# Gate and up products of a transformer block: weight blocks in the array and all 256 tokens moving, with norm pieces issued one tile ahead

## The chip, the core and the metric

The kernel runs on one core of one Trainium2 chip. A core has a matrix engine (PE in the profile; its loads of the stationary operand are listed apart as PEld), a vector engine (DVE), a scalar engine (ACT), a general engine (POOL) and a sync engine (SP), which here issues the transfers from memory. The metric is the device time of one execution in microseconds (us); lower is better. A matrix product holds one operand of 128x128 in the array (the stationary one, loaded by a LDWEIGHTS) and streams the other through it (the moving one, up to 512 columns); its result goes to an accumulator in PSUM.

## The reference

It is one block of a conformer-like transformer on 256 tokens of width 2048, all in float32:

```python
h = modulate(rms_norm(x, ffn1_norm), sh1, sc1)
x = x + 0.5 * g1[:, None, :] * swiglu(h, ffn1_w_gu, ffn1_w_down)
h = modulate(rms_norm(x, mix_norm), shm, scm)
y = hybrid_mixer(h, cos, sin, w_in, ...)        # differential attention and a causal convolution
x = x + gm[:, None, :] * y
h = modulate(rms_norm(x, ffn2_norm), sh2, sc2)
x = x + 0.5 * g2[:, None, :] * swiglu(h, ffn2_w_gu, ffn2_w_down)

def swiglu(h, w_gu, w_down):
    gu = jnp.einsum('bsd,df->bsf', h, w_gu)
    g, u = jnp.split(gu, 2, axis=-1)
    return jnp.einsum('bsf,fd->bsd', jax.nn.silu(g) * u, w_down)
```

The nine vectors of shifts, scales and gates come from one more product, of silu(c) with a matrix of 2048 x 18432 (`w_ada`). The inner width of swiglu is 5632.

## The kernel before

**Precision.** Every large product is made of three products of 32-bit operands: each operand is split into a high part that the array takes exactly and the rest (hi and lo), and hi x hi, hi x lo and lo x hi are added up in one accumulator (`mm3`, L311 to L316). Weights come from memory in tiles of 512 rows by 512 columns (1 MB, in `raw`); `w_tile` (L276) lets ACT make the high half (L293, `whi`) and DVE the rest (L295, `wlo`).

**A product tile.** `mm_tile` (L318) takes one weight tile. The activations are stationary: for each of the tile's 4 blocks of 128 rows and each of the 2 blocks of 128 tokens, `mm3` loads a 128x128 block of activations and moves 512 weight columns past it, three times: 24 instructions of 512 columns for one tile. There are 176 tiles of gate and up weights (22 chunks of 256 gate and 256 up columns, 4 tiles each, two FFNs), 88 of the down projections, 40 of `w_in` and 16 of `w_out`: 320 in all, 7680 instructions.

**Gate and up, then down.** `ffn` (L434) first takes the tiles of the first 512 rows for all chunks (`stage_a`, copied out by ACT at L461), since the norm of those rows is ready first; then some chunks further (`again`, `early`), and last the rest of each chunk. `finish` (L568) adds the parts of a chunk on DVE, applies SiLU on ACT, multiplies gate by up on DVE, and then has PE transpose the result, 4 blocks of 128x128 per chunk (L576), since the down product needs the inner columns on the partitions; ACT and DVE split the transposed result (L326, L327). `finish` of a chunk is issued after the first tile of the next chunk. The down products (L619 to L650) make 4 column groups of 11 tiles; the last `HOLD_DN` = 2 tiles of the last group are held so that the first 128 tokens come to an end before the others, and `evac` (L609) of these runs beside the products of the rest.

**Norms.** The normalized activations come in 4 pieces of 512 columns for each 128 tokens. `piece` (L396) scales on ACT (L364), and one tile later, or when a product first asks for it (`act`), `complete` (L409) lets PE transpose (L370), DVE or ACT apply scale and shift (L418, L421), and ACT and DVE split (L422, L423). In the FFNs `pieces` issues a piece once the modulation columns for it are there; in the mixer a piece is issued just before the first tile that needs it (L986).

**Order.** Each engine runs its instructions in a fixed order, which the framework's scheduler draws from the order of the code. The columns of `w_ada` are a transfer of 1 MB each and a multiply-and-sum on DVE (L180); the table `DUE` (L47) and the shares in the calls of `ffn` say how many of them lie between the weight tiles. `after_tiles` puts a step off by a number of tiles. `ORDER` (L48) is the order of the tiles of `w_out`.

Of the kernel before, what the change touches and what calls it, by code (L numbers as in the profile page):

```python
# [24 lines left out]
P = 128  # L25
# [21 lines left out]
DUE = ((19, 8), (63, 16), (110, 24), (150, 32))  # L47
ORDER = [(0, 0), (1, 0), (0, 1), (1, 1), (2, 0), (2, 1)] + [(n, pc) for pc in (2, 3) for n in range(3)]  # L48
# [25 lines left out]
def block_kernel(ctx: ExitStack, tc: tile.TileContext, x_in, pos_in, w_ada, small, w_gu1, w_dn1,  # L74
# [250 lines left out]
    def split_from_psum(tp, hi, lo):  # L325
        nc.scalar.copy(out=hi, in_=tp)  # L326
        nc.vector.tensor_sub(out=lo, in0=tp, in1=hi.bitcast(F32))  # L327
# [101 lines left out]


    HOLD = 3
    HOLD_DN = 2

    def ffn(st, w_gu, w_dn, gate_base, ada_a, ada_b, nxt, again, early, early_3):  # L434
# [20 lines left out]

        def stage_a(c, w, accs, ts, n=4):
            mm_tile(accs, w, act, 0, True, True, ts, (0, n))
            if parts[c] is None:
                parts[c] = blk([P, NT, 512])
            for t in ts:  # L460
                last_part[0] = nc.scalar.copy(out=parts[c][:, t, :], in_=accs[t])  # L461
# [10 lines left out]
        if not st.done:  # L472

            raws, begun = st.begin_both(), [0]
            ws = {}

            def load(i):
                cs = LOADS[i]
                if ext[cs[0]] == 1:
                    ws.update(zip(cs, w_first(cs)))  # L480
                else:
                    ws[cs[0]] = w_tile(w_gu[cs[0], 0], False, (0, ext[cs[0]]), ext[cs[0]] < 4)

            for c in range(NCH):
                ext[c] = EXT[c] if c < len(EXT) else 4
            def begin_ready():
                while begun[0] < 4 and base + 2 * begun[0] + 2 <= ada_next[0]:
                    st.tile(raws[begun[0]], tmp([P, S]), (begun[0], slice(0, S)))
                    begun[0] += 1

            first_modulation(lambda n: load(0) if n == 3 else None)
            begin_ready()
            for i in range(len(LOADS) + AHEAD):
                if i < len(LOADS):
                    if i:
                        load(i)
                    with tc.issue_after(w_dma[0].ins):
                        if i < len(FIRST_ADA):
                            ada_until(ada_next[0] + FIRST_ADA[i])
                            rows[0] += ext[LOADS[i][0]] * len(LOADS[i])  # L500
                        else:
                            ada_a_share(ext[LOADS[i][0]])
                        begin_ready()
                if i >= AHEAD:
                    cs = LOADS[i - AHEAD]
                    assert begun[0] >= ext[cs[0]]
                    for c in cs:
                        stage_a(c, ws[c], [acc_tile() for _ in range(NT)], (0, 1), ext[c])
                    pieces()
        else:  # L510
            first = [(c, w_tile(w_gu[c, 0], c > 0), [acc_tile() for _ in range(NT)]) for c in range(3)]
            for t in range(NT):
                for c, w, accs in first:
                    stage_a(c, w, accs, (t,))
            with tc.issue_after(st.last.ins):
                ada_a_share(12)
            for c in range(3, NCH):
                w = w_tile(w_gu[c, 0])
                stage_a(c, w, [acc_tile() for _ in range(NT)], (0, 1))
                ada_a_share(4)  # L520
                pieces()
# [6 lines left out]
        def add_part(c, accs):  # L528
            for t in range(NT):
                nc.vector.tensor_add(out=parts[c][:, t, :], in0=accs[t], in1=parts[c][:, t, :])  # L530

        start_of = [0] * NCH
        for g in again:
            w = w_tile(w_gu[g, 0], False, (ext[g], 4))
            accs = [acc_tile() for _ in range(NT)]
            mm_tile(accs, w, act, 0, True, True, (0, 1), (ext[g], 4))
            ext[g] = 4
            add_part(g, accs)
            ada_a_share(3)
        for i_g, g in enumerate(early):  # L540
# [5 lines left out]
            for c in g:  # L546

                accs[c] = [acc_tile() for _ in range(NT)]
                begun_[c] = ext[c] < 4
                if ext[c] < 4:  # L550
                    w = w_tile(w_gu[c, 0], False, (ext[c], 4))
                    mm_tile(accs[c], w, act, 0, True, False, (0, 1), (ext[c], 4))
                    ada_a_share(4 - ext[c])
                    ext[c] = 4
            for c in g:
                upto = 3 if c in early_3 else 2
                for pc in range(1, upto):
# [3 lines left out]
                    mm_tile(accs[c], w, act, 4 * pc, pc == 1 and not begun_[c], pc == upto - 1)  # L561
# [6 lines left out]
        def finish(c, accs):  # L568
            p = parts[c]
# [8 lines left out]
            split_from_psum(tp, a[:, 0], a[:, 1])  # L578
# [4 lines left out]
        for g in groups:  # L583
            accs = {c: [acc_tile() for _ in range(NT)] for c in g}
            for i, (pc, ks) in enumerate(segments(g[0], start_of[g[0]], 4)):
                ada_until(base + 8 * pc + 8)
                pieces(last_part[0])
                for c in g:
                    w = w_tile(w_gu[c, pc], False, ks)
                    mm_tile(accs[c], w, act, 4 * pc, i == 0, pc == 3, (0, 1), ks)  # L590
# [17 lines left out]

        def evac(n, accs, ts=(0, 1)):  # L609
            for t in ts:  # L610
                m = tmp([P, 512])
# [8 lines left out]
        for n in range(4):  # L620
            accs = [acc_tile() for _ in range(NT)]
            held = []
            for pc in range(11):
                hold = n == 3 and pc >= 11 - HOLD_DN
                w = w_tile(w_dn[n, pc], hold and pc == 10)
# [94 lines left out]


    ffn(norm1, w_gu1, w_dn1, 32, (0.78, 32), (0.8, 104), norm_m, AGAIN, EARLY, EARLY_3)


# [139 lines left out]
    def attn_av(g, qb, hh_):  # L864
# [10 lines left out]
        if hh_ == 3:  # L875
# [22 lines left out]
            after_tiles(1, rest)  # L898
# [80 lines left out]
    for t in range(NT):  # L979
        for c, w, accs in first:  # L980
            mm_tile(accs, w, act, 0, True, False, (t,))
    for ci in range(10):
        p0 = 1 if ci < HOLD else 0
        accs = first[ci][2] if ci < HOLD else [acc_tile() for _ in range(NT)]
        for pc in range(p0, 4):
            for t in range(NT):  # L986
                st.piece(pc, t)
# [45 lines left out]
    for i, (n, pc) in enumerate(ORDER):  # L1033
# [105 lines left out]
```

## Time and profile before

| | |
|---|---|
| median of 3 runs | 1875.45 us (1874.09 to 1875.72) |
| the profiled execution | 1871.77 us |
| its span, first to last instruction | 1870.0 us |
| granted TensorE clock, mean | 0.996 |
| DVE busy | 1436.1 us (77%) |
| ACT busy | 917.8 us (49%) |
| memory traffic | 495.93 MB, mean 265 GB/s |

The profile is of one execution. An instruction's row has its line in the code, engine, operation, output and inputs by the program's names, partitions x elements, the count, and after the bar the busy time in us, the mean of one in ns and the idle time of its engine ahead of it with what ended it. The end of a product is modelled, and products overlap in the array, so their pace is read from the distances of their starts and not from their durations. A timeline row has the start and the duration in us, the engine, the line, and in brackets a wait and what ended it. "x4" merges four rows that follow each other.

### The profile page before, as it was taken

To read this page: it belongs to the slowest core of one execution; us is meant where nothing else is said; L and a number is where in the kernel's file an instruction comes from. 1 tells how busy PE (TensorE), PEld (TensorE's weight loads), DVE (VectorE), ACT (ScalarE), POOL (GpSimd) and SP (SyncE) were. 2 spreads that over 40 slices of the span, in tenths; PEclk is the share of its full clock that TensorE was granted. 3 is DMA by queue.
4 is the path that set the end of the run, shared out by engine and by line. 5 is a ranking of instruction groups with operands and counts; after the bars stand their busy time and mean duration, and the time that the engine had idled before them with its cause. 6 is when DMAs were issued, how large, how long until landed. Compare 5 with 4: busy or idle time off the path is not lost.

```text
span 1870.0 us, 21989 instructions
## 1 busy us (share of the span) xinstructions
PE 1836.9 (98%) x8303; PEld 1512.4 (81%) x8303; DVE 1436.1 (77%) x1902; ACT 917.8 (49%) x1390; POOL 31.3 (2%) x29
## 2 busy tenths in 40 slices
PE   7999999999999999999999999999999999999999
PEld 5778888888887888788888788887888888888887
DVE  7788969999888788769899688788877755544443
ACT  6654344444444434654787455664444444433332
POOL 0000000000000000000110000000000000000000
PEclk9999999999999999999999999999999999999999
DMA  9887978988889899635444476888777755555562
GB/s 383 320 323 275 361 261 310 339 315 333 328 332 352 326 376 355 256 133 189 174 152 142 151 280 271 332 318 336 259 286 276 285 197 180 192 213 206 199 213 79
DMA packets 72586, 495.93 MB, mean 265 GB/s; under 512 B 8176, under 2 KB 8352, under 8 KB 15008
## 3 DMA queue, kind: packets, MB, share of 16 engines
q1 hardware_dynamic: 72480, 494.53, 70.8%
q8 instruction: 65, 1.06, 0.2%
q14 instruction: 41, 0.34, 0.0%
HBM read 492.37 MB, written 2.12 MB: 264 GB/s over the span
## 4 chain that ended last, share of the span: by engine, by line
PE 91%; DVE 3%; DMA 3%; ACT 1%; issue 1%; POOL 0%; SPq 0%; POOLq 0%; ACTq 0%; DVEq 0%
PE acc L315 29%; PE acc L316 29%; PE acc L314 29%; DMA blk<-in_w_gu_dram 1%; PE tp L576 1%; DVE wlo L295 1%; DMA raw<-in_w_ada_dram 1%; PE acc L834 1%; DVE blk L742 1%; DMA raw<-in_w_dn_dram 1%; DVE raw L180 0%; PE tp L370 0%; ACT whi L293 0%; PE tp L909 0%; POOL rs L141 0%
## 5 line engine op out<-in xcount | busy, mean ns | idle before, releaser
L293 ACT CAST whi<-raw 128x1024 fp32r<-128x1024 f32 (+1 forms) x609 | 632.4, 1047 | 765.8 <-PE acc L316 607.2
L314 PE MATMUL acc<-whi,blk 128*128 128x512 f32 x2464 | 963.7, 394 | 6.5 <-ACT blk L379 2.7
L315 PE MATMUL acc<-wlo,blk 128*128 128x512 f32 x2464 | 964.6, 391 | 5.1 <-DVE wlo L295 5.1
L295 DVE TENSOR_TENSOR wlo<-raw,whi 128x1024 fp32r<-128x1024 f32 (+1 forms) x609 | 730.0, 1211 | 309.1 <-ACT whi L293 306.9
L316 PE MATMUL acc<-whi,blk 128*128 128x512 f32 x2464 | 962.2, 391 | 0.6 <-DVE blk L381 0.5
L315 PEld LDWEIGHTS acc<-wlo,blk 128*128 128x128 f32 x2464 | 464.5, 188 | 103.8 <-DVE wlo L295 9.8
L314 PEld LDWEIGHTS acc<-whi,blk 128*128 128x128 f32 x2464 | 464.1, 189 | 104.3 <-ACT whi L293 3.4
L316 PEld LDWEIGHTS acc<-whi,blk 128*128 128x128 f32 x2464 | 463.9, 188 | 99.1 <-DVE blk L381 2.0
L180 DVE CUSTOM_DVE_ANT_0 raw<-raw,c_bc 128x2048 f32<-128x2048 f32 x142 | 324.3, 2284 | 10.0 <-DMA raw<-in_w_ada_dram 9.5
L742 DVE SCALAR_TENSOR_TENSOR blk<-blk,cst,blk 128x255 f32<-128x255 f32 (+14 forms) x240 | 96.3, 458 | 0.0
L461 ACT COPY blk<-acc 128x512 f32<-128x512 f32 x88 | 49.9, 591 | 51.1 <-PE acc L316 49.0
L572 DVE TENSOR_TENSOR blk<-acc,blk 128x512 f32<-128x512 f32 x88 | 56.9, 682 | 1.7 <-PE acc L316 1.6
L314 PE MATMUL acc<-blk,blk 128*128 128x512 f32 x96 | 38.4, 403 | 2.1 <-ACT blk L422 2.1
L315 PE MATMUL acc<-blk,blk 128*128 128x512 f32 x96 | 38.0, 400 | 0.2 <-DVE blk L295 0.2
L316 PE MATMUL acc<-blk,blk 128*128 128x512 f32 x96 | 37.6, 396 | 0.0
L573 ACT ACTIVATE blk<-blk 128x256 f32<-128x256 f32 x88 | 32.8, 410 | 5.4 <-DVE blk L572 5.4
L574 DVE TENSOR_TENSOR blk<-blk 128x256 f32<-128x256 f32 x88 | 33.9, 417 | 1.4 <-ACT blk L573 1.4
L612 DVE TENSOR_TENSOR tmp<-acc,blk 128x512 f32<-128x512 f32 x16 | 10.7, 686 | 27.7 <-PE acc L316 27.7
L295 DVE TENSOR_TENSOR blk<-raw,blk 128x1024 fp32r<-128x1024 f32 x24 | 28.8, 1219 | 2.9 <-ACT blk L293 2.9
L327 DVE TENSOR_TENSOR blk<-tp,blk 128x512 fp32r<-128x512 f32 x44 | 29.9, 683 | 0.5 <-ACT blk L326 0.2
L421 ACT ACTIVATE tmp<-tp,ada,scales 128x128 f32<-128x128 f32 x48 | 18.9, 460 | 20.9 <-DVE scales L222 14.5
L530 DVE TENSOR_TENSOR blk<-acc,blk 128x512 f32<-128x512 f32 x36 | 23.8, 685 | 6.5 <-PE acc L316 6.4
(144 smaller groups left out, 682.3 us busy)
## 6 DMA issues: line engine op xcount, KB each, us to landing
raw<-in_w_gu_dram SPq DMA_DIRECT2D x161, 1024.0 KB, 5.4
raw<-in_w_ada_dram SPq DMA_DIRECT2D x142, 1024.0 KB, 6.3
raw<-in_w_dn_dram SPq DMA_DIRECT2D x88, 1024.0 KB, 5.0
raw<-in_w_in_dram SPq DMA_DIRECT2D x40, 1024.0 KB, 4.8
raw<-in_w_out_dram SPq DMA_DIRECT2D x16, 1024.0 KB, 4.7
raw<-in_w_gu_dram SPq DMA_DIRECT2D x8, 768.0 KB, 6.0
blk<-in_w_gu_dram SPq DMA_DIRECT2D x10, 512.0 KB, 13.9
blk<-gate_line SPq DMA_DIRECT2D x6, 512.0 KB, 6.6
```

Source lines behind the costliest of these rows:

```text
L180: nc.vector.tensor_tensor_reduce(out=raw, in0=raw, in1=c_bc, scale=1.0, scalar=0.0, op0=ALU.mult, op1=ALU.add, accum_out=ada_cols[g][:, j ...
L293: nc.scalar.copy(out=hi[:, :m, :], in_=rw)
L295: nc.vector.tensor_sub(out=lo[:, :m, :], in0=rw, in1=hi[:, :m, :].bitcast(F32))
L314: nc.tensor.matmul(acc, ah, wh, start=start, stop=False)
L315: nc.tensor.matmul(acc, ah, wl, start=False, stop=False)
L316: nc.tensor.matmul(acc, al, wh, start=False, stop=stop)
L327: nc.vector.tensor_sub(out=lo, in0=tp, in1=hi.bitcast(F32))
L461: last_part[0] = nc.scalar.copy(out=parts[c][:, t, :], in_=accs[t])
L572: nc.vector.tensor_add(out=p[:, t, :], in0=accs[t], in1=p[:, t, :])
L573: nc.scalar.activation(out=p[:, t, :256], in_=p[:, t, :256], func=AF.Silu)
L574: nc.vector.tensor_mul(out=p[:, t, 256:], in0=p[:, t, :256], in1=p[:, t, 256:])
L742: nc.vector.scalar_tensor_tensor(out=y[:, d:], in0=u, scalar=w, in1=y[:, d:], op0=ALU.mult, op1=ALU.add)
```

## The change

`mm_tile_wide` and `mm3_wide` are new: the weight tile is cut into 128x128 blocks, each of them is loaded into the array, and all 256 tokens move. A tile then takes 48 instructions of 256 columns instead of 24 of 512; an accumulator holds gate or up columns as [128 columns, 2 blocks, 256 tokens]. All of the first FFN and chunks 3 to 21 of the second go this way (164 of the 176 tiles); chunks 0 to 2 of the second FFN stay as before. `finish` then needs no transposes in 41 of the 44 chunks. Beside that:

- `act_wide` asks for a norm piece of both token blocks at once; `pieces` is called in two more places, and the mixer issues the next piece ahead of each of its first tiles.
- `HOLD_DN` is 3, `DUE` has the columns of `w_ada` a little earlier, the share behind it is 0.78 for 0.8.
- The order of the `w_out` tiles is plain (row group by row group), and the transposes of the second half of the heads are put off by two tiles.
- `evac_last`: the last 128x512 block of the output is evacuated and written in two halves.

```diff
-DUE = ((19, 8), (63, 16), (110, 24), (150, 32))
-ORDER = [(0, 0), (1, 0), (0, 1), (1, 1), (2, 0), (2, 1)] + [(n, pc) for pc in (2, 3) for n in range(3)]
+DUE = ((19, 8), (55, 16), (107, 24), (150, 32))
...
+    def mm3_wide(acc, w, a, start, stop):
+        wh, wl = w
+        ah, al = a
+        for i, (w_, a_) in enumerate(((wh, ah), (wh, al), (wl, ah))):
+            nc.tensor.matmul(acc, w_, a_, start=start and i == 0, stop=stop and i == 2, skip_group_check=True)
+
+    def mm_tile_wide(accs, w, act, k0, start, stop, ks=(0, 4)):
+        for j in range(*ks):
+            wh, wl = w(j)
+            a = act(k0 + j)
+            for f in range(4):
+                fs = slice(f * P, (f + 1) * P)
+                mm3_wide(accs[f // 2][:, f % 2, :], (wh[:, fs], wl[:, fs]), a,
+                         start and j == ks[0] and f % 2 == 0, stop and j == ks[1] - 1)
+        tick()
...
+        def act_wide(self, k):
+            for t in range(NT):
+                self.complete(k // 4, t)
+            return self.hh[k // 4][:, k % 4, :], self.hl[k // 4][:, k % 4, :]
...
-    HOLD_DN = 2
+    HOLD_DN = 3
...
+        by_token = range(0 if base == 0 else 3)
...
         for g in again:
...
             ada_a_share(3)
+            pieces(last_part[0])
...
         def finish(c, accs):
+            if c not in by_token:
+                gate_, up = (part_of(c, i) for i in range(2))
+                nc.vector.tensor_add(out=gate_, in0=accs[0], in1=gate_)
+                nc.scalar.activation(out=gate_, in_=gate_, func=AF.Silu)
+                nc.vector.tensor_add(out=up, in0=accs[1], in1=up)
+                nc.vector.tensor_mul(out=up, in0=gate_, in1=up)
+                a = blk([P, 2, 2, S], F32R)
+                split(up, a[:, 0], a[:, 1])
+                aT[c] = a
+                return
...
+        def evac_last(n, acc, t):
+            for h in range(2):
+                cs = slice(256 * h, 256 * h + 256)
+                m = tmp([P, 256])
+                nc.vector.tensor_mul(out=m, in0=acc[:, cs], in1=gbc[n][:, cs])
+                nc.vector.tensor_add(out=x[n][:, t, cs], in0=x[n][:, t, cs], in1=m)
+                nc.sync.dma_start(out=out[t * P:(t + 1) * P, n * 512 + 256 * h:n * 512 + 256 * h + 256],
+                                  in_=x[n][:, t, cs])
...
-            after_tiles(1, rest)
+            after_tiles(1 + g, rest)
...
         for c, w, accs in first:
             mm_tile(accs, w, act, 0, True, False, (t,))
+            if t == 1 and c == 0:
+                for tt in range(NT):
+                    st.piece(1, tt)
...
-            for t in range(NT):
-                st.piece(pc, t)
+            if ci == 0 and pc < 3:
+                for t in range(NT):
+                    st.piece(pc + 1, t)
...
-    for i, (n, pc) in enumerate(ORDER):
+    for i, (n, pc) in enumerate([(n, pc) for pc in range(4) for n in range(3)]):
```

**On PE, inside a gate and up chunk.** First the kernel before, in the second FFN, where `finish` of one chunk falls between two blocks of the next chunk's tile. The row reads: output <- moving operand, stationary operand; `blk` in the third place is a block of activations, `tp` the transposed output of a finished chunk.

```order
L314 MATMUL acc_11142<-whi_11149,blk_9549 128x512
L315 MATMUL acc_11142<-wlo_11151,blk_9549 128x512
L316 MATMUL acc_11142<-whi_11149,blk_9550 128x512
L576 MATMUL tp_11177<-cst,blk_9461 128x128 x4
L314 MATMUL acc_11141<-whi_11193,blk_10002 128x512
L315 MATMUL acc_11141<-wlo_11195,blk_10002 128x512
L316 MATMUL acc_11141<-whi_11193,blk_10003 128x512
```

The same in the changed kernel, inside a chunk of the first FFN (L329 is the line of `mm3_wide`, `blk_2824` and `blk_2825` are the high and low parts of the activations):

```order
L329 MATMUL acc_4322<-blk_2824,whi_4394 128x256
L329 MATMUL acc_4322<-blk_2825,whi_4394 128x256
L329 MATMUL acc_4322<-blk_2824,wlo_4396 128x256
L329 MATMUL acc_4323<-blk_2824,whi_4394 128x256
L329 MATMUL acc_4323<-blk_2825,whi_4394 128x256
```

The two operands have changed places, the moving one has 256 columns, each instruction has a load of its own as before, and no row of L576's kind is left between tiles.

**On PE, at the start of the mixer.** Before: the transposes of the second norm piece (`tp_6032`, `tp_6051`) stand directly ahead of the first product that needs what ACT and DVE make of them (`blk_6016`, `blk_6017`).

```order
L314 MATMUL acc_5943<-blk_5938,blk_5827 128x512
L315 MATMUL acc_5943<-blk_5940,blk_5827 128x512
L316 MATMUL acc_5943<-blk_5938,blk_5828 128x512
L370 MATMUL tp_6032<-cst,tmp_6018 128x128 x4
L370 MATMUL tp_6051<-cst,tmp_6020 128x128 x4
L314 MATMUL acc_5918<-blk_6024,blk_6016 128x512
L315 MATMUL acc_5918<-blk_6026,blk_6016 128x512
```

In the changed kernel (L388 are these transposes, L313 to L315 are `mm3`; `blk_7943` is the new piece):

```order
L314 MATMUL acc_7882<-blk_7879,blk_7766 128x512
L315 MATMUL acc_7882<-blk_7877,blk_7767 128x512
L388 MATMUL tp_7961<-cst,tmp_7945 128x128 x4
L388 MATMUL tp_7977<-cst,tmp_7947 128x128 x4
L313 MATMUL acc_7894<-blk_7885,blk_7766 128x512
...
L315 MATMUL acc_7894<-blk_7889,blk_7767 128x512
L313 MATMUL acc_7881<-whi_8173,blk_7943 128x512
L314 MATMUL acc_7881<-wlo_8175,blk_7943 128x512
```

The 12 products of `acc_7894` now stand between the transposes and the first use of their result.

**On PE, at the first norm pieces of the first FFN.** Before, the transposes of the second piece (`tp_1030`, `tp_1049`) and of the third (`tp_1559`, `tp_1575`) come together:

```order
L316 MATMUL acc_991<-whi_994,blk_145 128x512
L370 MATMUL tp_1030<-cst,tmp_1016 128x128 x4
L370 MATMUL tp_1049<-cst,tmp_1018 128x128 x4
L370 MATMUL tp_1559<-cst,tmp_1521 128x128 x4
L314 MATMUL acc_936<-whi_1022,blk_1014 128x512
```

In the changed kernel the second piece stands ahead of a product that still uses the first one (`blk_144`); the third comes some 600 rows later:

```order
L329 MATMUL acc_1227<-blk_144,wlo_1224 128x256
L388 MATMUL tp_1264<-cst,tmp_1212 128x128 x4
L388 MATMUL tp_1280<-cst,tmp_1214 128x128 x4
L329 MATMUL acc_1304<-blk_144,whi_1296 128x256
L329 MATMUL acc_1304<-blk_145,whi_1296 128x256
```

Both steps are moved away from the product that waits for them.

More of the change, by code (lines that the diff above doesn't have):

```diff
@@ L518, in ffn @@
                 w = w_tile(w_gu[c, 0])
-                stage_a(c, w, [acc_tile() for _ in range(NT)], (0, 1))
+                stage_a(c, w, gu_accs(c), (0, 1))
                 ada_a_share(4)
@@ L528, in add_part @@
         def add_part(c, accs):
-            for t in range(NT):
-                nc.vector.tensor_add(out=parts[c][:, t, :], in0=accs[t], in1=parts[c][:, t, :])
+            for i in range(2):
+                nc.vector.tensor_add(out=part_of(c, i), in0=accs[i], in1=part_of(c, i))
         start_of = [0] * NCH
@@ L546, in ffn @@
             for c in g:
-                accs[c] = [acc_tile() for _ in range(NT)]
+                accs[c] = gu_accs(c)
                 begun_[c] = ext[c] < 4
@@ L577, in finish @@
             a = blk([P, 2, 2, S], F32R)
-            split_from_psum(tp, a[:, 0], a[:, 1])
+            split(tp, a[:, 0], a[:, 1])
             aT[c] = a
@@ L583, in ffn @@
         for g in groups:
-            accs = {c: [acc_tile() for _ in range(NT)] for c in g}
+            accs = {c: gu_accs(c) for c in g}
             for i, (pc, ks) in enumerate(segments(g[0], start_of[g[0]], 4)):
```

46 lines of the change are left out of this document (29 added, 17 removed).

## Prediction

> **What bounds the kernel now.** I read the head of the page and the shares of the chain that ended last first, then the groups by line, then timelines of PE in a quiet stretch, and last the stretches in which PE is not full.
>
> ```profile
> span 1870.0 us, 21989 instructions
> PE 1836.9 (98%) x8303; PEld 1512.4 (81%) x8303; DVE 1436.1 (77%) x1902; ACT 917.8 (49%) x1390; POOL 31.3 (2%) x29
> PE 91%; DVE 3%; DMA 3%; ACT 1%; issue 1%; POOL 0%; SPq 0%; POOLq 0%; ACTq 0%; DVEq 0%
> ```
> ```profile
> L314 PE MATMUL acc<-whi,blk 128*128 128x512 f32 x2464 | 963.7, 394 | 6.5 <-ACT blk L379 2.7 <-ACT whi L293 2.0 <-ACT blk L461 1.2
> L315 PEld LDWEIGHTS acc<-wlo,blk 128*128 128x128 f32 x2464 | 464.5, 188 | 103.8 <-DVE wlo L295 9.8
> ```
> ```profile
> 299.71 0.39 PE L316 MATMUL acc<-whi,blk 128*128 128x512 f32 x1
> ...
> 305.83 0.39 PE L316 MATMUL acc<-whi,blk 128*128 128x512 f32 x1
> ```
>
> PE holds 91% of the chain, and its instructions are the three of the large products. Between the two timeline rows lie 27 steps, (305.83 - 299.71) / 27 = 0.2267 us for 512 columns. The 7680 products at that pace are 1741 of 1870 us. So a change pays if it takes instructions or waits from PE, or changes this pace; what it does to ACT and DVE counts only where PE waits for them.
>
> **The pace of a 256-column product.** This term decides. The change makes 3936 products of 512 columns into 164 x 48 = 7872 of 256, each with a load of its own: the same columns, twice the loads. No row of before has 256 columns, so I bound it by the nearest rows.
>
> ```profile
> 410.62 0.40 PE L316 MATMUL acc<-whi,blk 128*128 128x512 f32 x1
> 410.63 0.59 PEld L576 LDWEIGHTS tp<-cst,blk 128*128 128x128 f32 x4
> 410.86 0.60 PE L576 MATMUL tp<-cst,blk 128*128 128x128 f32 x4
> 411.19 0.19 PEld L314 LDWEIGHTS acc<-whi,blk 128*128 128x128 f32 x1
> 411.21 0.48 PE L314 MATMUL acc<-whi,blk 128*128 128x512 f32 x1
> 411.30 0.19 PEld L315 LDWEIGHTS acc<-wlo,blk 128*128 128x128 f32 x1
> 411.53 0.40 PE L315 MATMUL acc<-wlo,blk 128*128 128x512 f32 x1
> 411.76 0.39 PE L316 MATMUL acc<-whi,blk 128*128 128x512 f32 x1
> 411.99 0.40 PE L314 MATMUL acc<-whi,blk 128*128 128x512 f32 x1
> ```
> ```profile
> L576 PE MATMUL tp<-cst,blk 128*128 128x128 f32 x176 | 26.1, 273 | 0.0
> ```
> ```profile
> 1058.64 3.77 PEld L909 LDWEIGHTS tp<-tmp,blk 128*128 128x128 f32 x32
> ```
> ```profile
> L909 PEld LDWEIGHTS tp<-tmp,blk 128*128 128x128 f32 x64 | 8.8, 213 | 0.2
> ```
>
> The reported 188 ns of a load is not its price. The load of L314 starts at 411.19 and the next at 411.30: 110 ns apart, since L314 started to stream in between. Four transposes of 128 columns take 0.60 us, of which 0.273 is the last: (0.60 - 0.27) / 3 = 109 ns for a load and its product. With one moving column (L909) it is (3.77 - 0.21) / 31 = 115 ns, a short pause among them. So 1 or 128 columns hide behind a load of about 110 ns: load and stream run beside each other, and the pace is the longer of the two. The **lower bound** for 256 columns is this load, 109 ns. For the **upper bound** let a product cost a fixed part a and b per column: a + 512 b = 226.7 and a + 128 b at most 109, so b is at least 0.3065, a at most 69.8, and 256 columns at most 148 ns. Were there no fixed part, it would be half the row of 512, 113.3 ns. I take **113.8**: it lies nearest to the rows on both sides, half the 512-column row and the 109 to 115 ns of the load-bound rows, with 0.5 ns for two streams that are now nearly equally long. Against before: 7872 x 0.5 ns = **+4 us** (bounds -34 and +273 us).
>
> One row speaks for a fixed part. In its first microseconds of products PE is slower:
>
> ```profile
> 21.48 0.63 PE L315 MATMUL acc<-wlo,blk 128*128 128x512 f32 x1
> 21.91 0.63 PE L316 MATMUL acc<-whi,blk 128*128 128x512 f32 x1
> 22.33 0.63 PE L315 MATMUL acc<-wlo,blk 128*128 128x512 f32 x1
> 22.76 0.53 PE L316 MATMUL acc<-whi,blk 128*128 128x512 f32 x1
> ```
>
> That is (22.76 - 21.48) / 3 = 427 ns, and not twice 226.7 = 453. If the array then streams at half its later rate, 512 columns take 213.3 at the full rate, and 13.3 ns of the 226.7 are something that doesn't stretch with the array. Whether it comes once per product or along with the columns, no row tells; it is the main rival below.
>
> **The transposes** that go are 41 groups of four. From L316 at 410.62 to L314 at 411.99 lie four products, 4 x 0.2267 = 0.91, and one group: 1.37 - 0.91 = 0.46 us. 41 x 0.46 = **-19 us**, all of it on PE's path. ACT's and DVE's part of `finish` stays about as long and PE no longer waits for it: a chunk's result is first read by the down product, for the last chunk ten tiles later.
>
> **The norm pieces and the order.** The rows in which PE stands for more than a microsecond, behind the start, and the stretches around them:
>
> ```profile
> 123.95 0.66 PE L370 MATMUL tp<-cst,tmp 128*128 128x128 f32 x4 [1.58 <-ACT tmp L421]
> ```
> ```profile
> 789.82 0.50 PE L314 MATMUL acc<-blk,blk 128*128 128x512 f32 x1 [2.07 <-ACT blk L422]
> ```
> ```profile
> 1034.39 1.10 PE L888 MATMUL tp<-cst,tmp 128*128 128x128 f32 x4 [1.75 <-ACT tmp L883]
> ```
> ```profile
> 1272.64 0.50 PE L315 MATMUL acc<-wlo,blk 128*128 128x512 f32 x1 [1.46 <-DVE wlo L295]
> ```
> ```profile
> 118.00:130.00 12.00, 10.22 (x46) 8.08 (x45) 11.03 (x17) 7.57 (x13) 0.00 (x0) 0.86 0.99 390
> 764.00:790.00 26.00, 22.70 (x103) 17.30 (x102) 21.37 (x38) 19.28 (x33) 2.01 (x2) 1.00 0.58 212
> 1020.00:1040.00 20.00, 17.70 (x94) 14.53 (x93) 16.50 (x40) 13.02 (x38) 5.38 (x4) 1.00 0.30 106
> ```
>
> PE is idle for 1.8, 3.3 and 2.3 us of these three. At 124 us two norm pieces come together and the second waits for ACT; now one comes at a time, ahead of products on the old piece: -2, and the granted clock, 0.86 in this stretch, should stay up, another -1. At 790 twelve products (2.7 us) now lie between the transposes and their use, more than the 2.07 waited; at 767 the third held tile gives the norm of the first tokens 2.7 us more of cover: together -3. At 1034 the last heads' transposes are put off by two tiles: -2. The wait at 1272 is for a weight split that stands behind additions on DVE; nothing in the change clears it. Sum **-8 us** (0 to -12; an earlier `w_ada` column can cost as much as it gives, since DVE is busy 11.03 of 12 us at 118, with SP's queue behind it).
>
> **The end.** After the last product come a multiplication, an addition and the transfer.
>
> ```profile
> 1865.53 0.69 DVE L612 TENSOR_TENSOR tmp<-acc,blk 128x512 f32<-128x512 f32 x1 [4.02 <-PE acc L316]
> 1866.25 0.69 DVE L613 TENSOR_TENSOR xall<-xall,tmp 128x512 f32<-128x512 f32 x1
> ```
> ```profile
> L574 DVE TENSOR_TENSOR blk<-blk 128x256 f32<-128x256 f32 x88 | 33.9, 417 | 1.4 <-ACT blk L573 1.4
> ```
>
> In halves that is 4 x 0.417 = 1.67 for 1.38 us, with the second transfer half as long: 0, between -1 and +0.3. The third held tile occupies buffers that nothing asks for at that point: 0.
>
> **The sum.** 1871.77 (profiled execution; 1.77 of it lie around the span) + 4 - 19 - 8 = 1848.8. The median of the runs lies 3.7 above that execution, so I predict **1852 us**, 1.2% faster.
>
> **A rule of the Trainium skill against the change.** The Trainium skill, "TensorE: Matmul & The Clock Gate", section "The mechanism" (of packing small matmuls), says that a load overlaps running products only when it goes to other row groups of the array. These loads fill all 128 rows, so load and product would follow each other; the trace disagrees, 109 ns for both of a transpose.
>
> **The rivals.**
> - *A fixed part per product.* If the 13.3 ns come once per product (a hand-over between two products, or the load taking turns with the stream), then 256 columns cost 213.3 / 2 + 13.3 = 120.0 ns, and 7872 x 6.67 = +52 us outweigh -27: 1875.45 + 52 - 27 = **1900, slower than before**. It decides from 27 / 7872 = 3.4 ns over 113.3. For it speaks the 427 ns row; against it, that the load-bound pairs hand over at 109 to 115 ns. Chance 0.37. The Trainium skill, "TensorE: Matmul & The Clock Gate", section "Back-to-back issue gap", gives a product N/2.4 ns plus a fixed 2.5, so 215.7 for 512 columns; the trace has 226.7, and by that column rate the other 13.3 would be fixed too.
> - *Something between*, 115 to 118 ns: 1862 to 1885; its middle is no change, its lower half faster. Chance 0.09.
> - *Load and product in turn*, 109 + 113 = 222 ns: 7872 x 0.109 = +858, some 2700 us. The transposes' row excludes it nearly: 0.01.
> - *The norm pieces don't do what they say*, and only the transposes go: 1860, inside the forecast's range.
>
> **How the numbers follow.** Forecast (113.3 to 115 ns, other gains 0 to -12): chance 0.53, 1844 to 1869. About 0.2% (3.7 us) is what a measurement of this kernel can tell from no change. Faster: 0.53 and 0.04 of the middle, 0.57; same 0.04; slower 0.39. The cases of both signs hold much, so the range reaches from the forecast's lower end to the rival's: **1840 to 1904**, leaving out a gain from everything at once and a rival with waits of its own.
>
> **What would show it.** In the changed profile the distance of starts of the 256-column rows in a quiet stretch: 113 to 115 right, 120 the rival; twelve of them, a block of 128 weight rows, take 1.37 us or 1.44. PE rows of transposes 12 in place of 176. At the first FFN's second norm piece and the mixer's start no PE wait above 1 us. PEld's busy share loses its meaning, since the loads will overlap one another. The forecast is wrong if PE waits for loads, or if a gap over 2 us opens where none was.

## The result and the profile after

| | before | after |
|---|---|---|
| median | 1874.93 us (1874.09 to 1875.72, 4 runs) | 1916.49 us (1914.95 to 1920.28, 4 runs) |
| profiled execution, its span | 1871.77, 1870.0 us | 1920.28, 1918.5 us |
| granted TensorE clock, mean | 0.996 | 0.989 |

The changed kernel is slower: ratio 1.0229, 95% interval [1.0209, 1.0249]. The forecast was 1852 us with a range to 1904; the time lies 12 us above that range, on the side of the rival with a fixed part per product.

The head of the page of after, the shares of the chain that ended last, the larger of the two groups of new products, and the group of the transposes that are left (the columns are those of the rows of before):

```profile
span 1918.5 us, 29533 instructions
PE 1878.7 (98%) x12075; PEld 1713.8 (89%) x12075; DVE 1436.6 (75%) x1863; ACT 912.7 (48%) x1349; POOL 32.3 (2%) x29
...
PE 89%; DVE 6%; DMA 2%; ACT 2%; issue 1%; POOL 0%; SPq 0%; DVEq 0%; ACTq 0%
...
L329 PE MATMUL acc<-blk,whi 128*128 128x256 f32 x5248 | 950.5, 284 | 8.0 <-ACT blk L500 3.5
```
```profile
L627 PE MATMUL tp<-cst,blk 128*128 128x128 f32 x12 | 1.7, 277 | 0.0
```

PE bounds it as before, and its share of busy time is the same 98%. The transposes have gone down from 176 to 12 as planned. So the time is in the products themselves; their pace stands in a quiet stretch of PE's timeline:

```profile
299.59 0.28 PE L329 MATMUL acc<-blk,whi 128*128 128x256 f32 x1
299.71 0.28 PE L329 MATMUL acc<-blk,wlo 128*128 128x256 f32 x1
299.83 0.40 PE L329 MATMUL acc<-blk,whi 128*128 128x256 f32 x2
300.07 0.28 PE L329 MATMUL acc<-blk,wlo 128*128 128x256 f32 x1
...
301.99 0.28 PE L329 MATMUL acc<-blk,whi 128*128 128x256 f32 x1
```

From 299.59 to 301.99 lie 20 products: 2.40 / 20 = **0.1200 us**, where 0.1138 was forecast and 0.1200 named for the rival. Of the 7862 distances between two such starts in the trace, 7693 are 120 ns. 7872 x (120.0 - 113.33) = **+52.5 us**, more than the whole difference.

The rest of the change shows at three stretches, in the windows view of after (length, busy time and count of PE, PEld, DVE, ACT and POOL, then the granted clock, the share of DMA, GB/s) and in the waits (in all, times, longest):

```profile
118.00:130.00 12.00, 12.00 (x103) 12.00 (x102) 10.08 (x15) 6.69 (x12) 0.00 (x0) 1.00 0.79 290
785.00:795.00 10.00, 7.12 (x24) 4.83 (x24) 6.12 (x13) 3.64 (x9) 0.55 (x1) 0.78 0.29 107
1055.00:1080.00 25.00, 22.11 (x91) 18.94 (x90) 15.16 (x28) 7.75 (x13) 0.00 (x0) 0.73 0.24 84
```
```profile
PE acc L314 <- DVE wlo L294: 7.0, 5, 2.9
...
PE tp L388 <- DVE tmp L380: 3.8, 2, 2.3
...
PE acc L313 <- ACT blk L440: 2.1, 1, 2.1
```

At 118 us PE is full and the clock at 1.00 (before: 10.22 of 12 us, 0.86): that wait is gone. At 785 (the mixer's first norm, at 764 in before) and at 1055 (`w_out`) PE stands, and the clock is down.

### The profile page after: what moved, and what is told of

It is laid out like the page before. It is cut to its first block, busy times and chain, and to the rows that moved or that the text cites. A ratio compares the mean times of both kernels' runs of the same rounds, so it can differ in the third digit from the quotient of the medians.

```text
span 1918.5 us, 29533 instructions
## 1 busy us (share of the span) xinstructions
PE 1878.7 (98%) x12075; PEld 1713.8 (89%) x12075; DVE 1436.6 (75%) x1863; ACT 912.7 (48%) x1349; POOL 32.3 (2%) x29
## 4 chain that ended last, share of the span: by engine, by line
PE 89%; DVE 6%; DMA 2%; ACT 2%; issue 1%; POOL 0%; SPq 0%; DVEq 0%; ACTq 0%
PE acc L329 47%; PE acc L314 13%; PE acc L315 13%; PE acc L313 13%; DVE wlo L294 1%; DVE blk L345 1%; DMA raw<-in_w_ada_dram 1%; DVE blk L806 1%; DVE raw L179 1%; PE acc L898 1%; DMA blk<-in_w_gu_dram 1%; PE tp L973 1%; PE tp L388 0%; ACT whi L292 0%; DVE blk L294 0%
## 5 line engine op out<-in xcount | busy, mean ns | idle before, releaser
L329 PE MATMUL acc<-blk,whi 128*128 128x256 f32 x5248 | 950.5, 284 | 8.0 <-ACT blk L500 3.5
L329 PEld LDWEIGHTS acc<-blk,whi 128*128 128x128 f32 x5248 | 821.8, 193 | 9.8 <-ACT blk L500 4.1
L329 PE MATMUL acc<-blk,wlo 128*128 128x256 f32 x2624 | 743.6, 284 | 2.2 <-DVE wlo L294 1.9
L329 PEld LDWEIGHTS acc<-blk,wlo 128*128 128x128 f32 x2624 | 505.4, 193 | 3.0 <-DVE wlo L294 2.5
L314 PE MATMUL acc<-wlo,blk 128*128 128x512 f32 x1136 | 447.9, 394 | 7.1 <-DVE wlo L294 7.0
L313 PE MATMUL acc<-whi,blk 128*128 128x512 f32 x1136 | 446.3, 396 | 3.5 <-ACT blk L440 2.1
L315 PE MATMUL acc<-whi,blk 128*128 128x512 f32 x1136 | 446.7, 394 | 0.6 <-DVE blk L399 0.5
L314 PEld LDWEIGHTS acc<-wlo,blk 128*128 128x128 f32 x1136 | 215.7, 190 | 54.4 <-DVE wlo L294 10.6
L313 PEld LDWEIGHTS acc<-whi,blk 128*128 128x128 f32 x1136 | 216.0, 190 | 49.5 <-ACT blk L440 2.4
L315 PEld LDWEIGHTS acc<-whi,blk 128*128 128x128 f32 x1136 | 215.4, 190 | 46.9 <-DVE blk L399 1.7
L315 PE MATMUL acc<-blk,blk 128*128 128x512 f32 x112 | 43.9, 392 | 0.0
L314 PE MATMUL acc<-blk,blk 128*128 128x512 f32 x112 | 43.7, 393 | 0.0
L313 PE MATMUL acc<-blk,blk 128*128 128x512 f32 x112 | 43.5, 395 | 0.0
L292 ACT CAST blk<-raw 128x1024 fp32r<-128x1024 f32 x28 | 29.2, 1060 | 7.1 <-DMA raw<-in_w_dn_dram 5.7
```

What stands on the lines that cost most here:

```text
L292: nc.scalar.copy(out=hi[:, :m, :], in_=rw)
L313: nc.tensor.matmul(acc, ah, wh, start=start, stop=False)
L314: nc.tensor.matmul(acc, ah, wl, start=False, stop=False)
L315: nc.tensor.matmul(acc, al, wh, start=False, stop=stop)
L329: nc.tensor.matmul(acc, w_, a_, start=start and i == 0, stop=stop and i == 2, skip_group_check=True)
```

## The experiments

Two questions were open: whether 120.0 ns belongs to the size of a product, to the exchange of the operands or to the load; and what the other edits do, from which 8 us were forecast. Ten kernels were run, each beside runs of the kernel before on its chip (medians 1875.24, 1874.66 and 1874.68 us in the three groups).

**The wide products alone** (`e1_wide_only`): the changed kernel with all other edits taken back.

```diff
-DUE = ((19, 8), (55, 16), (107, 24), (150, 32))
+DUE = ((19, 8), (63, 16), (110, 24), (150, 32))
-    HOLD_DN = 3
+    HOLD_DN = 2
-            pieces(last_part[0])
...
-                if nxt is None and n == 3 and t == 1:
-                    evac_last(n, accs[t], t)
-                    continue
...
-            after_tiles(1 + g, rest)
+            after_tiles(1, rest)
```

The second call of `pieces`, the mixer's pieces, the share of 0.8 and `ORDER` go back in the same way.

> Only the exchange of the operands in gate and up and the finish without transposes; norm pieces, held tiles, DUE, the w_out order and the last evacuation as before. Theory F (a 256-column product has a fixed 13.3 ns, 120.0 ns in all): 7872 x 6.67 = +52, 41 groups of transposes -19, so about 1875 + 33 = 1908 us, and some 3 us more for the lo splits on DVE that now pile up ahead of the down product, 1908 to 1912. Theory W (the wide form has large waits of its own, and the other edits give the 8 us that were forecast): 1920 to 1926.

Measured 1916.82 us (1914.91 to 1918.81), ratio 1.0227 [1.0212, 1.0243], pace 120.0 ns. So the wide products alone make up the loss. It lies between the two theories: 52.5 us for the pace, less 18.2 for 164 transposes at 111 ns (their starts lie 109 to 112 ns apart in the trace of before; by the 0.46 us of a group it would be 18.9), give 1875.2 + 34.3 = 1909.5. The 7.3 us that are left over are a remainder and not a sum of waits. Its trace has three waits of PE, 5.9 us in all, that stand again in `e8_wide_order_off` below; but its other waits differ from those of before too, in both directions: 3.25 us at 134 for 1.58 at 124, and nothing for the 1.46 at 1272.

**All the other edits alone** (`e2_rest_only`): the changed kernel with every chunk by token.

```diff
-        by_token = range(0 if base == 0 else 3)
+        by_token = range(NCH)
...
```

> All edits but the exchange: the 176 gate and up tiles keep activations in the array and 512 weight columns moving, with their transposes; norm pieces a tile ahead, three held tiles, DUE, w_out order and last evacuation as changed. If the pieces do what the prediction said: 1875 - 8 = 1867 us. Theory N (what they take from one wait they give back at others, and each wait over 1 to 2 us costs a stretch at half clock): 1872 to 1882.

Measured 1874.74 us (1871.01 to 1877.86, 10 runs), ratio 0.9997 [0.9986, 1.0009]: together they give nothing that can be told from no change.

**The size without the exchange** (`e3_cut256`): the kernel before, activations stationary, transposes kept, and each gate and up product of 512 weight columns cut into two of 256.

```diff
-        nc.tensor.matmul(acc, ah, wh, start=start, stop=False)
+        c0 = 0
+        for n in cuts:
+            s = slice(c0, c0 + n)
+            nc.tensor.matmul(acc[:, s], ah, wh[:, s], start=start and c0 == 0, stop=False, skip_group_check=True)
...
-                    mm_tile(accs[c], w, act, 4 * pc, i == 0, pc == 3, (0, 1), ks)
+                    mm_tile(accs[c], w, act, 4 * pc, i == 0, pc == 3, (0, 1), ks, cuts=(256, 256))
```

> The kernel before with every gate and up product of 512 weight columns cut into two of 256; activations stay in the array, transposes stay. Theory F: the price belongs to the size of the product, whichever operand is loaded: 176 tiles x 48 x 6.67 ns = +56 us, 1931 us, pace 120 ns. Rival: it belongs to the weights as stationary operand (loads that wait for ACT and DVE): pace 113 to 115 ns, 1875 to 1890 us.

Measured 1934.28 us (1930.51 to 1936.28), ratio 1.0324 [1.0307, 1.0341]. Its PE timeline in the quiet stretch, first and last of 28 products:

```profile
299.56 0.28 PE L317 MATMUL acc<-whi,blk 128*128 128x256 f32 x1
...
302.80 0.28 PE L317 MATMUL acc<-whi,blk 128*128 128x256 f32 x1
```

3.24 / 27 = 0.1200 us. The price is that of the size; which operand is stationary makes no difference to the pace.

**A ruler of sizes** (`e4_sizes`): the kernel before with the down products cut in 384 + 128 columns, most of `w_in` in 320 + 192, and in three of the four row groups of `w_out` two of four blocks with only 64 columns of activations loaded; there 64 of each 128 tokens are left out of the sum.

```diff
-                mm_tile(accs, w, a_act, 4 * pc, pc == 0, pc == 10)
+                mm_tile(accs, w, a_act, 4 * pc, pc == 0, pc == 10, cuts=(384, 128))
...
+                if pc > 0 and j in (1, 2):
+                    a_, acc = (a_[0][:, :64], a_[1][:, :64]), acc[:64, :]
```

> A ruler, not a candidate: the kernel before with down products cut 384 + 128 columns, most w_in products 320 + 192, and in the last three row groups of w_out the second and third block of each tile loading only 64 of 128 activation columns, which leaves out the other 64 tokens of each block there. Theory F (N/2.4 + 13.3 ns, a load of 110 ns beside it): 384 columns 173.3 ns, 320 columns 146.7, 128 and 192 columns 110 to 112 (the load), 512 columns with half the load still 226.7. Theory L (the 13.3 ns are the load taking turns with the stream): 512 columns with half the load 220.0. A cost along the columns: 384 columns 170.0, 320 columns 141.7.

Measured once: 2147.41 us. That total answers nothing here: PE waits 70.5 us, 38 times, for weight splits of DVE. The distances of starts do, first rows of the down product, then rows of `w_out` with their loads (PEld):

```profile
589.99 0.40 PE L317 MATMUL acc<-whi,blk 128*128 128x384 f32 x1
590.22 0.34 PE L318 MATMUL acc<-wlo,blk 128*128 128x384 f32 x1
590.40 0.34 PE L319 MATMUL acc<-whi,blk 128*128 128x384 f32 x1
590.57 0.22 PE L317 MATMUL acc<-whi,blk 128*128 128x128 f32 x1
590.63 0.27 PE L318 MATMUL acc<-wlo,blk 128*128 128x128 f32 x1
590.74 0.28 PE L319 MATMUL acc<-whi,blk 128*128 128x128 f32 x1
590.86 0.39 PE L317 MATMUL acc<-whi,blk 128*128 128x384 f32 x1
```
```profile
1261.67 0.39 PE L317 MATMUL acc<-whi,blk 128*64 128x512 f32 x1
...
1262.13 0.13 PEld L317 LDWEIGHTS acc<-whi,blk 128*64 128x64 f32 x1
...
1263.05 0.39 PE L317 MATMUL acc<-whi,blk 128*128 128x512 f32 x1
1263.06 0.19 PEld L318 LDWEIGHTS acc<-wlo,blk 128*128 128x128 f32 x1
```

Products of one size come in threes. The second and third of 384 columns take 0.35 us together. The first takes 0.23, and the first of 128 columns only 0.06, so at a change of size the starts are shifted; by what, no run shows. The medians of the trace (256 columns: of after and `e3_cut256`; 512 and 256 stand among products of their own size), beside 0.4167 ns per column + 13.3 (0.4167 is half of 426.7 / 512, from the half-clock row of the prediction):

| columns | 512 | 384 | 320 | 256 | 192 | 128 |
|---|---|---|---|---|---|---|
| second and third of three, ns | 227 | 175 to 176 | 147 | 120 | 113 | 111 to 112 |
| first of three, ns | 227 | 233 | 169 | 120 | 88 | 60 |
| by the fixed part | 226.7 | 173.3 | 146.7 | 120.0 | 93.3 | 66.7 |

The shifts nearly cancel: 11 rounds of three and three from 589.99 to 599.49 take 864 ns each, where 3 x 173.3 + 3 x 111.5 are 854. So down to 256 columns the fixed part holds within 3 ns in the second and third products, and below it the load does, at 111 to 113. A load of 64 columns is shorter (0.13 for 0.19 us) and leaves the 512-column product at (1263.05 - 1261.67) / 6 = 230 ns. So the 13.3 ns are not the load taking its turn, which would have shrunk with it. What else they are, no run shows. Every product here has a load of its own ahead of it, so a fixed part of the product can't be told from a fixed part of going over to the next loaded block.

**The norm pieces alone** (`e5_pieces_only`), **the order and the due times alone** (`e6_order_only`), **pieces and three held tiles** (`e7_pieces_hold`): each is the kernel before with those lines of the change; and the changed kernel without its order and due times (`e8_wide_order_off`). Their diffs are lines of the change shown above; of `e8_wide_order_off`:

```diff
-DUE = ((19, 8), (55, 16), (107, 24), (150, 32))
+DUE = ((19, 8), (63, 16), (110, 24), (150, 32))
...
-    ffn(norm1, w_gu1, w_dn1, 32, (0.78, 32), (0.78, 104), norm_m, AGAIN, EARLY, EARLY_3)
+    ffn(norm1, w_gu1, w_dn1, 32, (0.78, 32), (0.8, 104), norm_m, AGAIN, EARLY, EARLY_3)
...
-            after_tiles(1 + g, rest)
+            after_tiles(1, rest)
...
-    for i, (n, pc) in enumerate([(n, pc) for pc in range(4) for n in range(3)]):
+    for i, (n, pc) in enumerate([(0, 0), (1, 0), (0, 1), (1, 1), (2, 0), (2, 1)] + [(n, pc) for pc in (2, 3) for n in range(3)]):
```

> The kernel before with one part of the change alone: the norm pieces one tile ahead (first FFN's extra products and the mixer's start). All chunks by token, two held tiles, old order of w_out and old due times, old end. Theory P (the prediction's own terms): the waits at 124 us (1.58 us and a half-clock window of 3.4 us, 1.7 us lost by it) and at 790 us (2.07 us, and another such window) go, none opens: 5 us less, about 1870. Theory N (a wait that goes is replaced by one elsewhere, as in the run of all other edits together): 1873 to 1877. By N the trace shows a new PE wait above 1.7 us with a half-clock window behind it; by P none beyond those of before.

> The kernel before with the new order of w_out, the later draining of the last heads' share (1 + g) and the new due times alone. Theory P: the wait of 1.75 us at 1034 goes, 2 us less, 1873. Theory C (this part costs what the pieces give): the run of all other edits together waited 3.2 us at 1034 and its half-clock stretch behind was 13.7 us long, before's was 6.8 us, so 1.4 + 3.4 = 5 us more, about 1880, and its trace shows that wait again.

> The kernel before with the norm pieces one tile ahead and three held tiles; old order of w_out, old due times, old end. Theory P: 5 us of the pieces and 1 us at 767, about 1869. Theory C (order and due times took back what the pieces gave): the same 1869 to 1870, faster than both kernels. Theory N (each gain is replaced by a wait elsewhere): 1873 to 1877.

> The changed kernel (256-column products, pieces ahead, three held tiles, new end) with the old order of w_out and the old due times. Theory C: the wait of 2.9 us at 1062 and most of the 13.7 us at half clock behind it go, 1.4 + 3.4 to 7 us less than the changed kernel: 1909 to 1912. Theory N: 1915 to 1918, with another wait above 1.7 us in its place. Pace of a 256-column product 120.0 ns in both.

| | median, us | against before [95%] | to before, medians |
|---|---|---|---|
| pieces | 1865.97 (1862.96 to 1873.71) | 0.9959 [0.9943, 0.9975] | -8.7 |
| order and due times | 1879.16 (1877.07 to 1886.22) | 1.0034 [1.0021, 1.0047] | +4.5 |
| pieces and held tiles | 1867.14 (1864.01 to 1870.79) | 0.9957 [0.9944, 0.9969] | -7.5 |
| changed kernel without order and due times | 1907.08 (1906.84 to 1907.72) | 1.0174 [1.0161, 1.0187] | +32.4 |

The ratio is not that of the medians: by it the pieces give 7.7 us (4.7 to 10.7), and the order and the due times cost 6.4 (3.9 to 8.8). Theory C holds: two opposed parts. The three runs with the pieces came out 2 to 4 us below what was expected of them, and the order and the due times opened waits at 124 and 770 us (3.15 and 2.40 us) beside the one that was expected. The pieces do what the change says, and more than forecast. In the timeline of PE of `e5_pieces_only` around 124 us, where before stood 1.58 us, and in its windows:

```profile
122.25 0.60 PE L388 MATMUL tp<-cst,tmp 128*128 128x128 f32 x4
...
124.20 0.50 PE L313 MATMUL acc<-whi,blk 128*128 128x512 f32 x1 [0.41 <-ACT blk L440]
```
```profile
118.00:130.00 12.00, 11.59 (x58) 9.33 (x57) 11.00 (x17) 7.32 (x12) 0.00 (x0) 1.00 0.95 361
```
```profile
25.00:1036.00 1011.00, 999.40 (x4588) 823.18 (x4586) 872.24 (x1263) 525.58 (x900) 26.25 (x19) 1.00 0.76 285
```

0.41 us are left at 124, at 790 no wait is left, and the clock stays at 1.00 from 25 to 1036 us. The third held tile changes nothing beside the pieces that these runs could tell: 1867.14 and 1865.97 lie within each other's ranges. `e8_wide_order_off` can be foretold from the others: 1874.7 + 34.3 (pace and transposes) + 7.3 (the remainder of `e1_wide_only`) - 8.7 = 1907.6, measured 1907.08. This shows that the pieces give about as much in the wide kernel as in the kernel before; it doesn't show what the 7.3 are. The order and the due times thus cost the changed kernel 1916.5 - 1907.1 = 9.4 us, against 4.5 alone. Most of it is half-clock time: the mean granted clock of the four runs is 0.993 without them and 0.988 with them, and 0.005 x 1910 is 9.6 us (an estimate from these clocks). Some of the wide kernel's new waits stand in the waits of PE and two rows of the timeline of `e8_wide_order_off`:

```profile
PE acc L313 <- ACT blk L440: 2.1, 1, 2.1
```
```profile
547.66 0.50 PE L314 MATMUL acc<-wlo,blk 128*128 128x512 f32 x1 [2.19 <-DVE wlo L294]
...
552.21 0.50 PE L314 MATMUL acc<-wlo,blk 128*128 128x512 f32 x1 [1.53 <-DVE wlo L294]
```

Together 5.9 us. The first is a norm piece of the second FFN, and it isn't the wide form's alone: `e3_cut256`, with the activations stationary, waits 2.14 us there too. The two others stand at the first down products, and DVE's timeline of after has their cause, the same row as in `e8_wide_order_off`:

```profile
535.56 10.32 DVE L345 TENSOR_TENSOR blk<-blk,blk 128x512 fp32r<-128x512 f32 x17
545.79 1.22 DVE L294 TENSOR_TENSOR wlo<-raw,whi 128x1024 fp32r<-128x1024 f32 x1
```

17 low halves of finished chunks (the last line of `split`) come in one row ahead of a weight split that PE waits for. In the kernel before each of them reads a transpose, which PE makes chunk by chunk; that this kept them apart is an argument, and another place for them was not tried.

**Which half of the second part costs** (`e9_due_only`, `e10_wout_only`): the kernel before with the new due times, and with the new order of `w_out`.

```diff
-DUE = ((19, 8), (63, 16), (110, 24), (150, 32))
+DUE = ((19, 8), (55, 16), (107, 24), (150, 32))
-    ffn(norm1, w_gu1, w_dn1, 32, (0.78, 32), (0.8, 104), norm_m, AGAIN, EARLY, EARLY_3)
+    ffn(norm1, w_gu1, w_dn1, 32, (0.78, 32), (0.78, 104), norm_m, AGAIN, EARLY, EARLY_3)
```

> The kernel before with the new due times alone (the second and third column of the modulation weights earlier, and the earlier end of their second share in the first FFN). Order and due times together cost 4.5 us and opened waits at 124 us (3.15 us), 770 us (2.40 us) and 1043 us (2.92 us). Theory D (the due times shift DVE's and ACT's work ahead of the norm transitions): the waits at 124 and 770 belong to them, 1.6 + 2 us more than before and about 1.7 us for each half-clock window behind: 1877 to 1880 here. Theory O (the order of w_out costs it all): within 1 us of before, 1874 to 1876, with the waits of before alone.

> The kernel before with the new order of w_out and the later draining of the heads' share (1 + g) alone, old due times. Theory O: the 2.92 us wait at 1043 and the 1.2 us wait at 1134 are here, 4.5 us more than before: 1878 to 1881. Theory D: the wait at 1043 takes the place of the 1.75 us at 1034, about 1 us more: 1874 to 1877, and none above 1.7 us at 124 beyond that of before or at 770.

Measured 1877.81 us (1872.71 to 1885.49, 12 runs), 1.0018 [1.0003, 1.0033], for the due times; 1876.09 us (1873.03 to 1879.94, 12 runs), 1.0004 [0.9994, 1.0015], for the order, both inside what theory D expected. By medians these are 3.1 and 1.4 us, together the 4.5 of both. The intervals are wide, 0.6 to 6.2 us for the first and -1.1 to 2.8 for the second, which can't be told from nothing, so the sum is no proof. The rows with waits in PE's timelines, of the due times and of the order:

```profile
125.94 0.60 PE L314 MATMUL acc<-whi,blk 128*128 128x512 f32 x1 [2.19 <-ACT blk L422]
```
```profile
769.81 0.63 PE L370 MATMUL tp<-cst,tmp 128*128 128x128 f32 x4 [2.40 <-DVE tmp L362]
```
```profile
1040.24 0.50 PE L314 MATMUL acc<-wlo,blk 128*128 128x512 f32 x1 [2.91 <-DVE wlo L294]
```

The earlier columns of `w_ada` lengthen the wait at the first norm transition (2.19 us for 1.58) and open one of 2.40 us at the second; the plain order of `w_out`, with the later draining, has a wait of 2.91 us in place of the 1.75 at 1034. In DVE's timeline of after one sees behind what:

```profile
1053.51 7.84 DVE L806 SCALAR_TENSOR_TENSOR blk<-blk,cst,blk 128x236 f32<-128x236 f32 x21
1061.27 2.35 DVE L294 TENSOR_TENSOR wlo<-raw,whi 128x1024 fp32r<-128x1024 f32 x2
```

21 taps of the convolution stand ahead of the weight split that PE is waiting for.

## Why the prediction was wrong

- **What bounds the kernel** was right: PE, and within it the products.
- **The pace** is the step that failed: "I take 113.8: it lies nearest to the rows on both sides". It measured 120.0, +52.5 us for +4. Both bounds held (109 and 148), but nearness to the load-bound rows was the wrong guide. Those rows say only that a load takes about 110 ns; they say nothing of a product that streams longer than its load. The row that did, 427 ns at half clock against 226.7, was in the prediction and was given to the rival: 226.7 - 427 / 2 = 13.3 ns beside the columns. (That takes the 427 ns as columns alone. If the 13.3 ns "doesn't stretch with the array", as the prediction has it, it would be in the 427 too, and the two rows would give 2 x 226.7 - 427 = 26 ns, and 127 for 256 columns. The 213 ns of 256 columns at half clock, in the last section, show that nothing fixed is left there; no row of before showed it, so here the 120.0 had some luck.) The argument against it, "that the load-bound pairs hand over at 109 to 115 ns", was none, since 110 ns of load hide a short stream and its fixed part together. `e3_cut256` shows the 13.3 ns at 256 columns, `e4_sizes` within 3 ns at 320 and 384.
- **The transposes**: forecast -19; 164 x 111 ns = -18.2, with 12 of 176 left. Right. "PE no longer waits for it" was not: the low halves of `finish` now queue together ahead of the first down product, where PE waits 2.19 and 1.53 us. With these, 7.3 us of the wide kernel were not in the sum; the rest of them isn't accounted for. The prediction's own sign, a gap over 2 us where none was, showed in after at 547 (2.19), 790 (2.31, the mixer's first norm), 1062 (2.89) and 1343 us (2.14).
- **Norm pieces and order**, forecast -8, gave nothing together (`e2_rest_only`). At 124 and 790 us the forecast was -3 and -2 with the clock; the pieces alone gave -8.7. Mis-sized, because half-clock windows were counted at 124 only and too low: the two waits, 1.58 and 2.07 us, each had such a window behind it, 1.7 us more apiece, 7.1 in all; the other 1.6 us lie within the interval of the 8.7. At 767 the third held tile (-1) gave nothing. At 1034 (-2) the wait was replaced by a longer one. "An earlier `w_ada` column can cost as much as it gives" was in the text as a bound, and the due times cost 3.1 us (0.6 to 6.2) where they stand alone.
- **The end**: 0, right. From the last start of PE to the end of the span 4.9 us before (1870.0 - 1865.10) and after (1918.5 - 1913.64).
- **The rivals**: the fixed part per product was right in the pace. Of the two causes it named, the load taking turns is excluded by the 64-column load; the hand-over is what is left, and no run shows it apart. Its 1900 is 16 us short: 8 are the gain of the other edits that was counted and did not come, about 7 the remainder of the wide kernel. Load and product in turn is refuted, at 120 ns for both.

The account of the changed kernel by medians: 1874.9 + 52.5 - 18.2 + 7.3 - 8.7 = 1907.8, and the run without order and due times has 1907.1. With these the changed kernel has 1916.5. That the 9.4 us between are mostly half-clock time the granted clock shows; why they cost twice there is open. Of what was run, the kernel before with the pieces alone is the fastest, 1865.97 us, 0.4% below the kernel before; with the third held tile it is not told apart from that.

## What to carry to other kernels

Before cutting a product into smaller ones, count the products: here each costs 13.3 ns beside its columns, and a change that halves the columns must earn that back elsewhere. A row of the same product at half clock gave the fixed part here: its pace at full clock less half its pace at half clock. That holds because nothing fixed was left at half clock, which a second size there (213 and 427 ns for 256 and 512 columns) has to show first. Edits that move work between queues are to be timed one by one: a gain of 8.7 us and a loss of 4.5 alone looked like nothing together.

## What the hardware showed unexpectedly

**The granted clock goes in windows of 3.41 us, and a wait of about half a window is enough.** The windows view of before, cut along the changes of the clock (PE's busy time is the second number behind the range, the clock the last but two):

```profile
57.17:60.58 3.41, 1.79 (x9) 1.16 (x7) 0.64 (x3) 2.20 (x4) 0.00 (x0) 1.00 1.01 408
60.58:64.00 3.42, 2.89 (x12) 2.08 (x13) 3.42 (x4) 2.76 (x3) 0.00 (x0) 1.00 0.72 271
122.05:125.46 3.41, 1.63 (x10) 1.06 (x9) 3.41 (x6) 3.41 (x8) 0.00 (x0) 1.00 1.02 428
125.46:128.87 3.41, 3.41 (x12) 2.69 (x11) 3.27 (x8) 2.11 (x4) 0.00 (x0) 0.50 0.95 334
787.64:791.05 3.41, 1.34 (x6) 1.05 (x6) 0.74 (x2) 3.41 (x10) 0.00 (x0) 1.00 1.01 404
791.05:794.46 3.41, 3.41 (x9) 2.64 (x8) 1.63 (x2) 3.39 (x5) 0.00 (x0) 0.50 0.25 101
```

PE idle for 1.62 us of a window: the next one stays at 1.00. Idle for 1.78 or 2.07: the next one has 0.50, and 1.7 us are lost beside the wait. In the eleven traces of before, after and the experiments but the ruler, behind the first 25 us and apart from the windows of the next paragraph, a window at full clock with up to 1.88 us idle was followed by 1.00, and one with as little as 1.58 by 0.50, so the line lies between 1.6 and 1.9 us. The windows don't start with the wait, so the same wait costs this in one execution and not in another where it falls across two windows: the 2.07 us at 790 put 1.87 into one window in `e10_wout_only`, and the clock stayed at 1.00. The Trainium skill, "TensorE: Matmul & The Clock Gate", section "HAM oscillation — how this bites in real kernels", has as its rule no idle gaps of PE over some 3.4 us; the length of the window agrees, but here 1.8 us in one window are enough.

There are half-clock windows without any wait as well. Two more windows of before, and two rows of PE in after:

```profile
1040.23:1043.64 3.41, 3.41 (x28) 3.20 (x27) 2.68 (x6) 1.04 (x1) 0.00 (x0) 1.00 0.00 0
1043.64:1047.06 3.42, 3.42 (x15) 3.23 (x15) 1.10 (x2) 0.00 (x0) 0.00 (x0) 0.50 0.00 0
```
```profile
1065.65 6.83 PE L973 MATMUL tp<-tmp,blk 128*128 128x1 f32 x32
...
1083.73 3.63 PE L973 MATMUL tp<-tmp,blk 128*128 128x1 f32 x32
```

PE is full in the first of these windows, and from 1040.80 us most of it is transposes with one moving column (L909; L973 in after). In after such a series from 1083.73 is followed by 0.50 at 1087.49, again without a wait. The series at 1065.65 runs in the half-clock stretch behind the wait of 2.89 us, takes 6.83 us for 3.63, and the clock is back at 1.00 only 13.65 us after it fell. In before, the series at 1058.86 falls across the end of a window at 1060.71, and no half-clock window follows. One reading is that products of one column count as idle here; no run tests it. It would make this part of `w_out` a place where a longer wait costs more than itself.

**At half clock the fixed part is gone.** PE's timeline of after, in such a window:

```profile
68.65 0.63 PE L329 MATMUL acc<-blk,whi 128*128 128x256 f32 x2
...
69.29 0.63 PE L329 MATMUL acc<-blk,whi 128*128 128x256 f32 x2
```

Three products in 0.64 us, 213 ns each: half of the 427 of 512 columns. At full clock the two are 120.0 and 226.7. The Trainium skill, on the same page, section "Wait — 56ns, not 53.3ns?", states a fixed cost per product that shows only at full clock, of about 2.5 ns. The kind agrees with this trace, the size does not: 13.3 ns for these 32-bit products, each with a load ahead of it.
